# Sixty-four bytes: moving the norms' operands from 64 to 0 modulo 128 bytes in SBUF

## The chip, the cores and the metric

The kernel runs on 1 core of one Trainium2 chip. What counts is the device time of one execution in microseconds (us), lower being better. Engines are called TensorE (PE in the rows; PEld is its loading of stationary operands), VectorE (DVE), ScalarE (ACT), GpSimd (POOL) and SyncE (SP).

## The reference

Two transformer blocks over 256 tokens of width 1024, in float32. Block 1 has one layer: a mixer with three kinds of attention side by side, a gated MLP with a short convolution, and a gate on a second input `p`. Block 2 has two layers, each with a mixer (the first an mLSTM and stick-breaking attention, the second a gated delta network), a cross attention to a memory of 256 rows, and an MLP with a squared relu. Each part begins with an RMS norm with a gain.

```python
def first_block(x, p, ...):
    h = x
    hn = rms_norm(h, ln_mix[0])
    z = hn @ w_in[0]                       # split into q, k, v of 3 kinds of attention
    ...
    h = h + jnp.concatenate([o_a, o_b, o_c], axis=-1) @ w_out[0]
    h = h + conv_gated_mlp(rms_norm(h, ln_ffn[0]), w_up[0], conv_w[0], conv_b[0], w_down[0])
    gate = jax.nn.sigmoid(rms_norm(h, ln_ple[0]) @ w_ple_gate[0])
    return h + (p[0] @ w_ple_proj[0]) * gate

def second_block(x, mem, ...):
    memn = rmsnorm(mem, mem_norm)
    for l in range(2):
        h = rmsnorm(x, mix_norm[l])
        x = x + (ab_mixer(h, ...) if l == 0 else c_mixer(h, ...))
        x = x + mem_cross_attn(rmsnorm(x, xa_norm[l]), memn, xa_wq[l], xa_wk[l], xa_wv[l], xa_wo[l])
        x = x + sq_relu_mlp(rmsnorm(x, mlp_norm[l]), mlp_w1[l], mlp_w2[l])
    return rmsnorm(x, final_norm)
```

## The kernel before

All activations stay in SBUF, with features on the partitions: `h` is [128, 8, 256]. The weights (some 200 MB) stream in as chunks of 128 x 2048 floats (1 MB) in the order of their use. SyncE loads a chunk in two halves `raw`; ScalarE casts each into `hi` (float32r), VectorE or GpSimd makes the rest `lo` = raw - hi (`fetch`, line 433). A ring of three places holds `hi` and `lo`.

Every product of weights is made of three: hi x hi, hi x lo and lo x hi, each a product of 256 columns on a 128 x 128 stationary operand. A chunk is 48 such products. There are three ways to use a chunk:

- `gemm_a`: the weights are stationary, the activations move; result [columns, tokens] in a PSUM tile `pg`. In a trace its products read `pg<-oh,hi`, `pg<-ol,hi`, `pg<-oh,lo`: the moving operand stands first after the arrow, the stationary one second.
- `gemm_b`: the activations are stationary, the weights move; result [tokens, columns]: `pg<-hi,oh`, `pg<-lo,oh`, `pg<-hi,ol`.
- `gemm_c`: 256 rows of a weight, added up over the chunks in four tiles `acc`; the weights are stationary, the activations move: `acc<-oh,hi` and so on in the output projections, `acc<-mh,hi`, `acc<-mlo,hi` (`acc<-ml,hi` in block 1) in the MLPs' second products, `ph`/`plo` in `ple_p`.

The activations' two parts are `oh` and `ol`, 8 KB a partition each. `opnd` takes them from the pool `op` (two of each), for the norms' results, the memory's operand and the collected outputs of most mixers:

```python
    def opnd(self, pool=None):
        p = pool or self.op
        return (p.tile([128, 8, T], F32R, tag="oh", name="oh"), p.tile([128, 8, T], F32R, tag="ol", name="ol"))
```

Only the first mixer of block 2 takes its outputs' `oh` and `ol` from a pool of its own (line 1182, `ov = self.opnd(one)`), and there the gates' weights `gw` lie in that tile's first half too (line 1183); in the delta mixer (line 1382) both come from `op`.

In chunks, with an operand in `op`: attention of block 1 14, its output projection 4, gated MLP 22, last gate of block 1 4, first mixer of block 2 20, delta mixer 24 and its output projection 4, each cross attention 4 for queries and 4 for its output, each MLP of block 2 16. Of these 22 are used by `gemm_b`. The other chunks (the MLPs' second products, the first mixer's output projection, `ple_p`) move operands from other pools.

Order: TensorE runs its products in the order in which the program writes them. Attention and the recurrences are tasks that are written between the weights' products at places fixed by a table `W` of assumed times. The tile framework puts the other engines' work in order when the program is built.

Places: pools are stacked in SBUF in the order in which they are opened. The built program puts the tiles (bytes from the start of a partition) at:

```
pool            tiles              before              modulo 128
ring            hi, lo, raw        22720 to 88256      64
op              oh, ol             88256 to 121024     64
res             h                  121024 to 129216    64
sm              sq, u, R           129216 to 139456    64
later pools     mh, ml, mlo, ph,   from 140288         0
                plo, ov of ab_mixer
```

Of the kernel before, what the change touches and what calls it, by code (L numbers as in the profile page):

```python
# [19 lines left out]
# how long (us) a step beside the weight products waits for the other engines before the tensor engine takes it up  # L20
# [24 lines left out]
# ---------------------------------------------------------------- layout plan  # L45
def _plan():
    """Weight chunks of 128 x 2048 floats, in the order in which they are used."""
    ch = []

    def a(name, layer, cols):  # L50
        ch.append((name, layer, "A", cols))

    def c(name, layer, row):
        ch.append((name, layer, "C", row))

    idx = {}

    def mark(key):
        idx[key] = len(ch)

    sl = lambda s, n=256: [(s, n)]

    def kv(l, js):
        for j in js:
            for n in ("xa_wk_2", "xa_wv_2"):
                mark((n, l, j)); a(n, l, sl(256 * j))

    mark("va"); a("w_in", 0, sl(1024))
    for i in range(2):
        mark(("dqk", i, 0)); a("w_in", 0, [(128 * i, 128), (512 + 128 * i, 128)])  # L70
        mark(("dqk", i, 1)); a("w_in", 0, [(256 + 128 * i, 128), (768 + 128 * i, 128)])
    f0, c0 = 1280, 2438
    mark("vf0"); a("w_in", 0, sl(f0 + 768))
    for i in range(3):
        mark(("fqk", i)); a("w_in", 0, [(f0 + 128 * i, 128), (f0 + 384 + 128 * i, 128)])
        if i == 0:
            mark("vf1"); a("w_in", 0, [(f0 + 768 + 256, 128), (c0 + 768, 128)])
    for i in range(3):
        mark(("cqk", i)); a("w_in", 0, [(c0 + 128 * i, 128), (c0 + 384 + 128 * i, 128)])
        if i == 0:  # L80
            mark("vc1"); a("w_in", 0, sl(c0 + 768 + 128))
    for j in range(4):
        mark(("w_out", j)); c("w_out", 0, 256 * j)
    for j in range(22):
        mark(("w_up", j)); a("w_up", 0, [(128 * j, 128), (2816 + 128 * j, 128)])
        if j % 2 and j > 2:
            mark(("w_down", j // 2 - 1)); c("w_down", 0, 256 * (j // 2 - 1))
    mark(("w_down", 10)); c("w_down", 0, 2560)
    mark("ple_p"); c("w_ple_proj", 0, 0)
    for j in range(4):  # L90
        mark(("ple_g", j)); a("w_ple_gate", 0, sl(256 * j))
    kv(0, range(3))
    for j in range(2):
        mark(("mo", j)); a("ab_w_in_2", 0, sl(1024 + 256 * j))
    for j in range(2):
        mark(("sv", j)); a("ab_w_in_2", 0, sl(2568 + 256 * j))
    for h in range(4):
        mark(("sqk", h)); a("ab_w_in_2", 0, [(1544 + 128 * h, 128), (2056 + 128 * h, 128)])
    for j in range(2):
        mark(("mv", j)); a("ab_w_in_2", 0, sl(512 + 256 * j))  # L100
    for i in range(2):
        mark(("mqk", i)); a("ab_w_in_2", 0, [(128 * i, 128), (256 + 128 * i, 128)])
    kv(0, (3,))
    for j in (2, 3, 0, 1):
        mark(("ab_out", j)); c("ab_w_out_2", 0, 256 * j)
    for l in range(2):
        if l == 1:
            for g in range(2):
                for hh in range(4 * g, 4 * g + 4):
                    mark(("cqk2", hh)); a("c_w_in_2", 0, [(128 * hh, 128), (1024 + 128 * hh, 128)])  # L110
                for i in (2 * g, 2 * g + 1):
                    mark(("cv", i)); a("c_w_in_2", 0, sl(2048 + 256 * i))
            for j in range(4):
                if j == 3:
                    kv(1, range(4))
                mark(("cg", j)); a("c_w_in_2", 0, sl(3072 + 256 * j))
            for j in range(4):
                mark(("c_out", j)); c("c_w_out_2", 0, 256 * j)
        for j in range(4):
            mark(("xa_wq_2", l, j)); a("xa_wq_2", l, sl(256 * j))  # L120
        for j in range(4):
            mark(("xa_wo_2", l, j)); c("xa_wo_2", l, 256 * j)
        for j in range(16):
            mark(("w1", l, j)); a("mlp_w1_2", l, sl(256 * j))
            if j > 1:
                mark(("w2", l, j - 2)); c("mlp_w2_2", l, 256 * (j - 2))
        for j in (14, 15):
            mark(("w2", l, j)); c("mlp_w2_2", l, 256 * j)
    return ch, idx
# [15 lines left out]
# constants that depend on shapes alone: for the whole kernel, block 1, the first mixer  # L145
# [111 lines left out]
# ---------------------------------------------------------------- the program  # L257
class Task:
    """work beside the stream of weight products: a generator that yields how long its next step waits"""
# [5 lines left out]
class Prog:  # L265
    def __init__(self, ctx, tc, io):
# [3 lines left out]
        self.ring = pool("ring", 3)  # L270
        self.op = pool("op", 2)
        self.res = pool("res", 1)
# [14 lines left out]
    # -- order: the tensor engine runs what is traced as it is traced  # L287
# [14 lines left out]
    def wait(self, w):  # L302
        """a number, or the name of a wait: the next of its entries"""
        if not isinstance(w, str):
            return w or 0.0
        n = self.waits[w] = self.waits.get(w, -1) + 1
        v = W[w] if isinstance(W[w], tuple) else (W[w],)
        return v[min(n, len(v) - 1)]
# [6 lines left out]
    def queue(self, fn, wait=0.0, lanes=(0, 1)):  # L315
        """fn(lane) -> generator, when one of the lanes (two banks each) is free"""
        self.pend.append((fn, self.clk + self.wait(wait), lanes))
# [32 lines left out]
    # -- engines  # L350
# [32 lines left out]
    def three(self, out, l, r, start, stop):  # L383
        """a product of operands in two parts"""
# [9 lines left out]
    # -- banks  # L394
# [7 lines left out]
    def ps(self):  # L402
        """for work that is traced at one go"""
        self.psn = 1 - self.psn
        return self.bank(4 + self.psn)
# [26 lines left out]
    # -- weights  # L432
    def fetch(self, i, between=None):
        """the chunk's two parts; with between, in quarters, for the start"""
# [52 lines left out]
    def gemm_a(self, key, x):  # L487
        """[columns, tokens]: two tiles of columns"""
        return self.gemm_ab(key, x, False)

    def gemm_b(self, key, x):
        """[tokens, columns]: two tiles of tokens"""
        return self.gemm_ab(key, x, True)

    def gemm_c(self, key, xh, xl, acc, first, last, mid=None, banks=(0, 1, 2, 3)):
        """256 rows, accumulated over the chunks; with mid, the first 128 rows for all columns before it"""
# [14 lines left out]
    def gate_weights(self, i, w):  # L511
        """the gates' columns, two groups of heads at columns 0 and 32, as two parts side by side"""
# [8 lines left out]
    def gate_rows(self, x, w, out, tmp):  # L521
        """out [heads, groups, tokens] = the gates before their norm"""
# [10 lines left out]
    # -- norms: operands are h*g, the reciprocal root is applied to the products  # L533
# [4 lines left out]
    def split(self, x, k, src, n=1, eng=None):  # L538
        """x[:, k:k+n] = src (float32, SBUF or PSUM) as two parts"""
# [3 lines left out]
    def behind(self, last, pair):  # L543
        """the pair of instructions (of the scalar and the vector engine) comes after the names in last"""
# [11 lines left out]
    def norm(self, h, gain, add=None, cols=False, bank=None, pool_sq=()):  # L556
        """h (in place) += add; operands, R (broadcast over partitions) and R per token, whose task runs later"""
# [56 lines left out]
    def v_cols(self, dst, ps, rc):  # L614
        """dst(t) <- ps[:, t] * per token"""
# [3 lines left out]
    # ------------------------------------------------------------ setup  # L619
# [26 lines left out]
    def warm(self):  # L646
        """products that nothing uses, for the tensor engine's clock"""
# [5 lines left out]
    def last_norm(self, h, add, out):  # L653
        """the output: h += add, its norm, in tiles of two"""
# [29 lines left out]
    def log1pe(self, l, y, n):  # L684
        """l = ln(1 + exp(-|y|))"""
# [4 lines left out]
    # ------------------------------------------------------------ block 1  # L690
    def softmax(self, S, E, b0, b1, tag):
        """S: [q, 384] scores (128 keys of the first 128 queries, 256 of the others); E = exp(S + b - max); 1/sum"""
# [17 lines left out]
    def turn(self, pt, P):  # L710
        """P [q, 384] -> pt [keys, 384]"""
# [9 lines left out]
    def block1_attention(self, x, R, rc):  # L721
        nc, tc, io = self.nc, self.tc, self.io
        with ExitStack() as es:
# [94 lines left out]
            def post(key, gq_, gk_, then, bank):  # L818
                """the norms of a tile of queries and a tile of keys, then the attention with them"""
# [140 lines left out]
    def out_proj(self, keys, ov, tiles, there=None, halves=False):  # L960
        """the last chunk (or its second half) waits for all tasks"""
# [77 lines left out]
    # ------------------------------------------------------------ block 2  # L1039
# [19 lines left out]
    def mem_operand(self, x=None, last=None):  # L1059
        """the memory's operands"""  # L1060
# [8 lines left out]
    def kv(self, l, pool):  # L1069
        """keys and values of the memory; a closure for each head's chunks"""  # L1070
# [105 lines left out]
    def ab_mixer(self, x, R, rc, kv_head, *_):  # L1176
        nc, tc = self.nc, self.tc
        with ExitStack() as es:
# [13 lines left out]
            # gates of the mLSTM, heads on partitions  # L1192
# [12 lines left out]
            # output gates  # L1205
# [24 lines left out]
            # stick breaking  # L1230
# [46 lines left out]
            # mLSTM  # L1277
# [93 lines left out]
    def c_mixer(self, x, R, rc, kv_head, K, Vm):  # L1371
        nc, tc = self.nc, self.tc
        with ExitStack() as es:
# [7 lines left out]
            # the memory's operand, then the output's; the place of the memory's keys and values serves the convolutions before  # L1381
# [14 lines left out]
            def gates():  # L1396
                # beta and decays, heads on partitions
# [142 lines left out]
            def base(g, cpt):  # L1540
                # inverses of the 16 x 16 diagonal blocks, a block per partition
# [99 lines left out]
            def gated(j):  # L1641
                """heads 2 j, 2 j + 1: times their norms and gates, when both are there"""
# [59 lines left out]
    def blocks_out(self, N, cpt):  # L1702
        """N[(k b), r, c] = cpt[(b r), k, c]"""
# [4 lines left out]
    def blocks_in(self, ci, I):  # L1708
        """ci[(b r), k, c] = I[(k b), r, c]"""
# [62 lines left out]
```

## Time and profile before

| | |
|---|---|
| median of 3 runs | 1342.69 us (1340.6 to 1343.25) |
| profiled execution, its span | 1345.5 us; no other time of it is recorded |
| TensorE busy | 1280.4 us, 95% |
| VectorE, ScalarE, GpSimd busy | 924.7, 727.9, 274.7 us |
| weights' queue | 200.76 MB, 44.0% of the DMA engines' time |

The span runs from the first to the last instruction of the profiled execution. Busy time of TensorE counts overlapping products once. A product's own duration (some 0.28 us) runs from its start to the modelled end of its pipeline; the next product starts well before that end.

### The profile page before, as it was taken

The numbers are of one execution on the slowest core, as the hardware profiler recorded it, in microseconds if no ns is written. First come the engines' busy times: TensorE is split into PE (matmuls) and PEld (weight loads), VectorE is DVE, ScalarE is ACT, GpSimd is POOL, SyncE is SP. The second block draws the span as 40 slices with busy tenths as digits, with TensorE's granted clock in tenths as the row PEclk, the third lists the DMA queues.
The fourth block names the chain that finished last, engine by engine and source line by source line (L and its number), as shares of the span: only waits on it lengthen the run. The fifth ranks groups of instructions, "written<-read, shape, count | busy, mean of one in ns | idle before, by whom it ended". The sixth has DMA issues, their size and how long they took to land. (4 is left out here: it accounts for less than half of the span.)

```text
span 1345.5 us, 24944 instructions
## 1 busy us (share of the span) xinstructions
PE 1280.4 (95%) x10195; PEld 1238.7 (92%) x10195; DVE 924.7 (69%) x1401; ACT 727.9 (54%) x1217; POOL 274.7 (20%) x160
## 2 busy tenths in 40 slices
PE   8899989999999999999999999888898989999997
PEld 7788889999999999989999998778798989999997
DVE  7867687777786655686655657989685376755554
ACT  6665475655576554655444446564643564644442
POOL 4500330000223200262000015424214271100000
PEclk9999999999999999999999999999998989999999
DMA  8323445555565543434655555333234343455551
GB/s 267 135 98 108 140 165 188 177 182 182 181 205 185 173 152 128 155 130 140 211 180 184 182 184 170 137 92 109 94 110 131 110 141 122 161 188 186 183 184 45
DMA packets 65698, 208.40 MB, mean 155 GB/s; under 512 B 13192, under 2 KB 14752, under 8 KB 65584
## 3 DMA queue, kind: packets, MB, share of 16 engines
q1 hardware_dynamic: 56976, 200.76, 44.0%
q0 software_dynamic: 1600, 4.88, 1.1%
q10 hardware_dynamic: 7008, 1.18, 0.5%
q8 instruction: 80, 1.31, 0.4%
q14 instruction: 34, 0.28, 0.1%
HBM read 205.32 MB, written 1.44 MB: 154 GB/s over the span
## 5 line engine op out<-in xcount | busy, mean ns | idle before, releaser
L352 ACT ACTIVATE hi<-raw 128x1024 fp32r<-128x1024 f32 (+1 forms) x378 | 378.5, 1047 | 237.8 <-issue 101.9
L369 DVE TENSOR_TENSOR lo<-raw,hi 128x1024 fp32r<-128x1024 f32 (+1 forms) x311 | 378.2, 1250 | 171.7 <-ACT hi L352 171.3
L378 PE MATMUL pg<-oh,hi 128*128 128x256 f32 x1632 | 473.5, 290 | 9.2 <-DVE K L369 3.4
L378 PE MATMUL pg<-ol,hi 128*128 128x256 f32 x1632 | 466.2, 286 | 4.4 <-DVE ol L372 3.7
L378 PE MATMUL pg<-oh,lo 128*128 128x256 f32 x1632 | 464.0, 284 | 0.0
L378 PEld LDWEIGHTS pg<-oh,hi 128*128 128x128 f32 x1632 | 315.3, 193 | 14.2 <-issue 6.8
L378 PEld LDWEIGHTS pg<-ol,hi 128*128 128x128 f32 x1632 | 315.0, 193 | 10.1 <-DVE ol L372 8.3
L378 PEld LDWEIGHTS pg<-oh,lo 128*128 128x128 f32 x1632 | 315.0, 193 | 0.0
L369 POOL TENSOR_TENSOR lo<-raw,hi 128x1024 fp32r<-128x1024 f32 (+1 forms) x67 | 170.2, 2555 | 641.9 <-ACT hi L352 624.1
L378 PE MATMUL acc<-mh,hi 128*128 128x256 f32 x688 | 192.8, 280 | 0.6 <-ACT mh L352 0.6
L378 PE MATMUL acc<-mh,lo 128*128 128x256 f32 x688 | 192.0, 279 | 0.0
L378 PE MATMUL acc<-mlo,hi 128*128 128x256 f32 x512 | 142.8, 279 | 0.0
L378 PEld LDWEIGHTS acc<-mh,hi 128*128 128x128 f32 x688 | 129.3, 188 | 0.8 <-ACT mh L352 0.8
L378 PEld LDWEIGHTS acc<-mh,lo 128*128 128x128 f32 x688 | 129.3, 188 | 0.0
L378 PE MATMUL pg<-hi,oh 128*128 128x256 f32 x352 | 105.9, 301 | 5.4 <-DVE u L369 3.4
L378 PE MATMUL pg<-lo,oh 128*128 128x256 f32 x352 | 102.1, 290 | 1.5 <-DVE lo L369 1.4
L378 PE MATMUL pg<-hi,ol 128*128 128x256 f32 x352 | 101.8, 289 | 0.7 <-DVE ol L372 0.7
L378 PEld LDWEIGHTS acc<-mlo,hi 128*128 128x128 f32 x512 | 95.9, 187 | 0.0
L378 PE MATMUL acc<-oh,hi 128*128 128x256 f32 x320 | 91.6, 286 | 0.5 <-ACT oh L352 0.5
L378 PE MATMUL acc<-ol,hi 128*128 128x256 f32 x320 | 90.3, 282 | 0.1
L378 PE MATMUL acc<-oh,lo 128*128 128x256 f32 x320 | 90.2, 282 | 0.0
L369 POOL TENSOR_TENSOR sq<-sq 128x512 f32<-128x512 f32 (+1 forms) x20 | 26.7, 1337 | 261.8 <-ACT sq L352 260.5
(382 smaller groups left out, 1924.9 us busy)
## 6 DMA issues: line engine op xcount, KB each, us to landing
raw<-in_w SPq DMA_DIRECT2D x374, 512.0 KB, 4.2
mt<-in_memT POOLq DMA_DIRECT2D x12, 256.0 KB, 4.0
h<-in_xT SPq DMA_DIRECT2D x4, 256.0 KB, 4.9
raw<-in_w SPq DMA_DIRECT2D x4, 256.0 KB, 5.2
fl<-in_rel SPq DMA_DIRECT2D x3, 256.0 KB, 4.3
gw<-in_gw POOLq DMA_DIRECT2D x2, 256.0 KB, 2.9
out<-h SPq DMA_DIRECT2D x2, 256.0 KB, 2.7
con<-in_con SPq DMA_DIRECT2D x1, 384.0 KB, 7.0
```

The source lines that it names most:

```text
L352: return self.nc.scalar.activation(out, in_, func, **k)
L369: return (eng or self.nc.vector).tensor_tensor(out, a, b, op)
L378: i = self.nc.tensor.matmul(out, lhsT=l, rhs=r, start=start, stop=stop, skip_group_check=True)
```

## The change

Two tiles of 64 bytes a partition, each in a pool of its own, are allocated ahead of `op` and behind it. No instruction uses them. The rest of the change strips comments and docstrings, line for line, which moves nothing (and adds three lines ahead of line 274, so that later line numbers are 3 higher).

```diff
         self.cst = pool("cst", 1)
         self.ring = pool("ring", 3)
+
+        pool("gap0", 1).tile([128, 16], F32, name="gap0")
         self.op = pool("op", 2)
+        pool("gap1", 1).tile([128, 16], F32, name="gap1")
         self.res = pool("res", 1)
         self.sm = pool("sm", 2)
```

The places then are:

```
pool            tiles              after               modulo 128
ring            hi, lo, raw        22720 to 88256      64
op              oh, ol             88320 to 121088     0
res             h                  121152 to 129344    64
sm              sq, u, R           129344 to 139584    64
later pools     mh, ml, mlo, ...   from 140416         0
```

So `op` moves by 64 bytes, and everything behind it by 128. In the built programs each engine has the same instructions in the same order before and after.

## Rows read from the trace of the kernel before

**Rows 1.** Head of the page: busy us (share of the span) and instructions.
```profile
PE 1280.4 (95%) x10195; PEld 1238.7 (92%) x10195; DVE 924.7 (69%) x1401; ACT 727.9 (54%) x1217; POOL 274.7 (20%) x160
```

**Rows 2.** Busy time by stretch: attention, gated MLP, first mixer, MLP, delta mixer.
```profile
core 0: us, PE busy (x) PEld busy (x) DVE busy (x) ACT busy (x) POOL busy (x), PEclk, DMA share, GB/s
...
30.00:142.00 112.00, 106.71 (x750) 94.10 (x749) 83.36 (x193) 70.22 (x153) 23.58 (x16) 0.95 0.36 120
...
178.40:373.00 194.60, 191.79 (x1595) 190.55 (x1594) 154.03 (x229) 117.04 (x180) 19.05 (x15) 1.00 0.53 179
...
405.50:540.60 135.10, 135.10 (x1092) 132.74 (x1091) 78.03 (x103) 77.08 (x135) 17.60 (x9) 1.00 0.47 160
...
629.70:814.10 184.40, 183.82 (x1539) 183.16 (x1539) 112.58 (x124) 87.18 (x111) 15.51 (x8) 1.00 0.53 181
814.10:950.00 135.90, 116.98 (x869) 108.03 (x868) 120.09 (x206) 82.91 (x146) 56.18 (x27) 0.97 0.38 126
```

**Rows 3.** Waits of ScalarE: for whom, us in total, times, longest us.
```profile
ACT hi L352 <- PE pg L378: 93.9, 47, 9.0
```

**Rows 4.** Chain of waits, last MLP: start us, us, work, count.
```profile
1174.91 5.76 PE pg L378 x48
1180.67 5.66 PE acc L378 x48
```

**Rows 5.** Timeline of TensorE, output projection of the delta mixer: start us, us.
```profile
1068.03 0.28 PE L378 MATMUL acc<-oh,hi 128*128 128x256 f32 x1
...
1073.79 0.28 PE L378 MATMUL acc<-oh,hi 128*128 128x256 f32 x1
```

**Rows 6.** Timeline of TensorE, output projection of the first mixer.
```profile
550.16 0.28 PE L378 MATMUL acc<-oh,hi 128*128 128x256 f32 x1
...
551.93 0.28 PE L378 MATMUL acc<-oh,hi 128*128 128x256 f32 x1
```

**Rows 7.** Timeline of TensorE, weights moving, first mixer.
```profile
435.32 0.28 PE L378 MATMUL pg<-hi,oh 128*128 128x256 f32 x1
...
440.73 0.28 PE L378 MATMUL pg<-hi,oh 128*128 128x256 f32 x1
```

**Rows 8.** Timeline of TensorE, gates of the first mixer, then of the delta mixer.
```profile
441.08 0.28 PE L378 MATMUL ps<-oh 128*128 128x256 f32 x1
...
442.91 0.28 PE L378 MATMUL pg<-hi,oh 128*128 128x256 f32 x1
...
829.14 0.28 PE L378 MATMUL ps<-oh 128*128 128x256 f32 x1
...
830.77 0.28 PE L378 MATMUL pg<-oh,hi 128*128 128x256 f32 x1
```

**Rows 9.** Costliest groups of the page, loads: count, busy us, mean ns, idle before.
```profile
L378 PEld LDWEIGHTS pg<-oh,hi 128*128 128x128 f32 x1632 | 315.3, 193 | 14.2 <-issue 6.8
...
L378 PEld LDWEIGHTS acc<-mh,hi 128*128 128x128 f32 x688 | 129.3, 188 | 0.8 <-ACT mh L352 0.8
```

**Rows 10.** Groups of TensorE's products by operands: count, busy us, mean ns, idle.
```profile
L378 PE MATMUL pg<-oh,hi 128*128 128x256 f32 x1632 | 473.5, 290 | 9.2 <-DVE K L369 3.4 <-DVE u L369 2.6 <-DVE y L369 1.8
...
L378 PE MATMUL acc<-mh,hi 128*128 128x256 f32 x688 | 192.8, 280 | 0.6 <-ACT mh L352 0.6
...
L378 PE MATMUL acc<-mlo,hi 128*128 128x256 f32 x512 | 142.8, 279 | 0.0
L378 PE MATMUL pg<-hi,oh 128*128 128x256 f32 x352 | 105.9, 301 | 5.4 <-DVE u L369 3.4 <-ACT hi L352 1.1 <-ACT u L356 1.0
...
L378 PE MATMUL acc<-oh,hi 128*128 128x256 f32 x320 | 91.6, 286 | 0.5 <-ACT oh L352 0.5
...
L378 PE MATMUL acc<-ml,hi 128*128 128x256 f32 x176 | 49.3, 280 | 1.3 <-DVE ml L369 1.3
```

**Rows 11.** Groups of VectorE with shapes kept apart: count, busy us, mean ns, idle.
```profile
L372 DVE SCALAR_TENSOR_TENSOR cV<-cV,rq,u 128x128 f32<-128x128 f32 x16 | 4.6, 344 | 0.0
...
L372 DVE SCALAR_TENSOR_TENSOR om<-num,den,gg 128x128 f32<-128x128 f32 x8 | 2.2, 345 | 0.0
```

## The prediction

> **What bounds the kernel now.** The head of the page comes first: TensorE is busy 1280.4 of 1345.5 us, 95% [rows 1]. So the time is nearly that of one queue of products, and what one product takes is what counts. The stages then show where this holds without a gap. In the first MLP of block 2, its first mixer and the gated MLP of block 1 the busy time fills the stretch (183.82 of 184.40 us, 135.10 of 135.10, 191.79 of 194.60), while VectorE has 112.58, 78.03 and 154.03 us of work there. In the gated delta mixer it does not (116.98 of 135.90), and there VectorE is the busier one with 120.09; in the attention of block 1 TensorE has 106.71 of 112.00, at a granted clock of 0.95 [rows 2]. The weights are no limit: ScalarE's casts `hi` wait 93.9 us in total for products `pg`, that is for TensorE to free the three places of the ring, not the other way round [rows 3].
>
> Products overlap, so a row's own 0.28 us is not the price of a product; the distance from one start to the next is. The chain of waits, which merges unbroken work, gives it for a whole chunk: 48 products `pg` with the moving operand from `op` take 5.76 us, 120.0 ns each, and the 48 products `acc` of the chunks that follow take 5.66 us, 117.9 ns [rows 4]. Clock, shape (128x256 on a 128x128 stationary) and type are the same. The table of places in the section on the kernel gives one difference: in the first, both operands lie at 64 modulo 128; in the second, the moving one lies at 0 and the stationary one (the weights) at 64.
>
> **Is it the place, or the kind of product?** Four comparisons of the trace of before bear on it.
> First, the output projections. All run the same code. That of the delta mixer takes `ov` from `op` (64 against 64): from 1068.03 to 1073.79 us stand 48 products, 120.0 ns [rows 5]. That of the first mixer of block 2 takes `ov` from its own pool (0 against 64): from 550.16 to 551.93 stand 15, 118.0 ns [rows 6]. Same function, same weights' ring, 2 ns apart.
> Second, products in which the weights move and `oh` or `ol` is stationary (64 against 64): from 435.32 to 440.73 stand 45, 120.2 ns [rows 7].
> Third, the gates' products, moving `oh` and `ol` against a small weight tile. Where that tile lies in `op` (64 against 64), 14 take 1.63 us from 829.14, 116.4 ns; where it lies in the mixer's pool (64 against 0), 16 take 1.83 us from 441.08, 114.4 ns [rows 8]. Again 2 ns, and now it was the stationary operand that was moved.
> Fourth, the load of the stationary operand: 193 ns on average for `pg`, 188 for `acc` with `mh` [rows 9]. So it looks as if the load for the next product and the stream of the present one get in each other's way when they start at the same place modulo 128.
>
> The Trainium skill speaks against this: its page SBUF — State Buffer, section Who interferes with whom, gives TensorE two read ports, one for the moving operand and one for the load of weights, and calls them independent. By that the change would be worth nothing. Rows 5 and 6 differ by 2 ns all the same, and I go by the rows.
>
> **The change, part by part.** It adds no instruction and takes none away: both new tiles are written and read by nobody, and order and waits on every engine stay. What moves is `op` alone relative to everything else in the window of 128 bytes: `oh` and `ol` go from 64 to 0, while the ring, `h` and the later pools keep their place in it.
>
> Products that get faster: those with one operand in `op` and the other in the ring. The groups `pg` with `oh` or `ol` moving count 3 x 1632 = 4896, those with the weights moving 3 x 352 = 1056, and `acc` with `oh` or `ol` 3 x 320 = 960, less the 192 of the first mixer that already are at 0 [rows 10]. That is 6720, or 140 chunks of 48. Price: 5.76 - 5.66 = 0.10 us per chunk, so 14.0 us at most. For the 22 chunks in which the weights move, no row shows 64 against 0 with full-width loads; the nearest is the gates' 2.0 ns, so I price them like the others. Bounds for these 1056: nothing below (120 stays), and above, the gates' 114.4 ns, 5.8 ns each, 6.1 us instead of 2.2.
>
> Products that could get slower: the gates' 16 in the first mixer, now 0 against 0, cost 16 x 2 ns; nothing. The products `acc` with `mh`, `ml` or `mlo` keep 0 against 64 modulo 128, but every later pool moves by 128 bytes, so modulo 256 they change sides. They are 688 x 2 + 512 + 176 = 2064 [rows 10], with the first mixer's 192 and the 48 of `ple_p` 2304. Rows show no such pair, so the bounds are the ends seen: 114.4 and 120.2 ns against 117.9, from 8.1 us of gain to 5.3 us of loss. I take 0: the title's window is 128, and rows 8 show the same 2 ns from the other side of it.
>
> Other engines: 88 casts and as many subtractions of the norms write `op`, and VectorE reads `h` at 64 with `oh`, now at 0. Its product `om`, with inputs at 64 and 32, takes 345 ns, and `cV`, with both at 0, 344 [rows 11]; places that differ cost VectorE nothing.
>
> **What arrives at the end.** A chunk saved on TensorE counts only where TensorE is not waiting for others afterwards. By stages of [rows 2], in chunks with an operand in `op`:
> - gated MLP of block 1 (22) and the two MLPs of block 2 (16 each): 54 chunks with no wait to speak of; all of it, 5.4 us.
> - first mixer of block 2: 20 chunks, no gap at all; 2.0 us.
> - four output projections: 16 chunks, behind which the last attention steps are waited for; I take three quarters, 1.2 us.
> - attention of block 1 (14), its last gate (4), the queries of both cross attentions (8), the delta mixer (24): 50 chunks, 5.0 us. Here steps of VectorE and ScalarE are begun by one product and used by a later one; if the products between go faster, the later one waits longer by as much. TensorE idles in these stages already. I take half, 2.5 us.
> Sum 11.1 us; 2.9 of the 14.0 turn into longer waits for VectorE. The profiled execution has a span of 1345.5 us (no other time of it is known), which would become 1334.4. It lies 2.8 us above the median of the runs, 1342.7; from there the forecast is **1331.6 us**.
>
> **The rivals.**
> (a) No change. Either the reading ports don't meet, as the skill's page has it, or what makes `op` slow is its region and not its phase: it lies below byte 121,024, and all fast moving operands of other pools lie above 140,288. Rows 5 and 6 don't separate the two. Against the region: in rows 8 the moving operand is in `op` both times, and only the partner's place changes; but that partner also moves to the upper region. Then the time is 1342.7.
> (b) More than forecast. The 1056 products with weights moving fall to the gates' 114.4 ns (3.9 us more), and so may those of the later pools (8.1 us more): with the full 14.0 us, 1342.7 - 26.0 = 1316.7. For it speaks only that the gates' products, with half of their loads 64 wide, are quicker in every case (116.4 with equal places), so the level is more likely theirs alone.
> (c) Slower: the later pools. If 128 bytes put `mh`, `ml`, `mlo` and their like on a worse side against the weights, 2304 products pay. From 11.1 / 2304 = 4.8 ns each the gain is gone, and at 6 ns (the whole distance between the slowest and the fastest spacing seen) 13.8 us make 1345.4. The equal places cost only 2 ns, which speaks against it.
> (d) The gain is swallowed. All stages but the 54 plain chunks wait away what they save, and one of the gaps so lengthened brings the granted clock down once more. The 0.95 over 112.00 us stands for 5.6 us lost, in a stretch with waits [rows 2]; a third of that is 1.9. The time is then 1342.7 - 5.4 + 1.9 = 1339.2.
>
> **How the numbers follow.** A difference under about 0.2%, 2.7 us, is not told from none here. The forecast with its neighbours (4 to 18 us faster) gets 0.78; (a) 0.10; (b) 0.05; (c) 0.04; (d), as far as it eats nearly all, 0.03. Faster by over 0.2%: 0.78 + 0.05 and a little of (d), 0.84. Within: (a) and part of (c) and (d), 0.13. Slower: the rest of (c), 0.03. The range runs from the whole 14.0 us with 3.9 more for the moving weights (1324.8, so 1325) to (d) at 1339; outside it lie (a), most of (b) and (c), under two in ten.
>
> **What the profile after would show.** In the chain of waits, 48 products `pg` in 5.66 us like `acc`, or 5.76 if the step is wrong. The output projection of the delta mixer at 118 ns. Loads for `pg` at 188 instead of 193 ns. `acc` with `mh` still 5.66 us a chunk; more means (c). Longer waits of TensorE for VectorE in the delta mixer and the attention of block 1; the plain stretches shorter by 1.6 us for an MLP's 184.4 and 2.2 us for the gated MLP. The forecast is wrong if `pg` keeps its 120 ns, or if it reaches 118 and the waits grow by more than 2.9 us.

## The result and the profile after

The changed kernel takes 1332.56 us (median of 6 runs, 1327.06 to 1334.47), the kernel before in the same comparison 1342.97 us (1340.60 to 1348.09). The medians differ by 10.4 us; the ratio of the runs is 0.9911, 95% interval 0.9886 to 0.9936, which is some 12 us. Forecast were 11.1.

The profiled execution of the changed kernel is the fastest of its six (1327.06 us, span 1325.3). That of before has a span of 1345.5 us; since a span is 1.8 us shorter than the time in the runs that have both, it took some 1347.3 us (an estimate), 4.3 above its median. (The prediction set this span against a time, and so had 2.8; its forecast starts from the median and is not touched by it.) The two spans differ by 20.2 us, so stretches of the two traces differ by more than the medians do.

The head of the page, to [rows 1]: TensorE has 19.1 us less of busy time; every engine has the same number of instructions as before.

```profile
PE 1261.3 (95%) x10195; PEld 1220.8 (92%) x10195; DVE 922.0 (70%) x1401; ACT 727.8 (55%) x1217; POOL 276.1 (21%) x160
```

The chain of waits of the changed kernel in the last MLP, to [rows 4] (start us, us, work, count):

```profile
1150.46 5.65 PE acc L381 x48
1156.11 5.66 PE pg L381 x48
```

48 products `pg` take 5.66 us instead of 5.76; `acc` is where it was. The timeline of TensorE in the delta mixer's output projection, to [rows 5]: 36 products in 4.23 us, 117.5 ns instead of 120.0.

```profile
1055.09 0.28 PE L381 MATMUL acc<-oh,hi 128*128 128x256 f32 x1
...
1059.32 0.28 PE L381 MATMUL acc<-oh,hi 128*128 128x256 f32 x1
```

And with the weights moving, in the first mixer, to [rows 7]: 48 products in 5.44 us, 113.3 ns instead of 120.2.

```profile
440.89 0.28 PE L381 MATMUL pg<-hi,oh 128*128 128x256 f32 x1
...
446.33 0.28 PE L381 MATMUL pg<-hi,oh 128*128 128x256 f32 x1
```

The loads, to [rows 9]: 189 ns on average for `pg`, 193 before. Those of `acc<-mh,lo` went the other way, from 188 to 192 ns, though 48 products `acc` take 5.65 us as before. So a load's own duration does not follow the pace of the products. The first line is of before, the others of the changed kernel:

```profile
L378 PEld LDWEIGHTS acc<-mh,lo 128*128 128x128 f32 x688 | 129.3, 188 | 0.0
...
L381 PEld LDWEIGHTS pg<-oh,hi 128*128 128x128 f32 x1632 | 308.5, 189 | 11.9 <-issue 3.4 <-ACT hi L355 2.8 <-ACT K L359 1.8
...
L381 PEld LDWEIGHTS acc<-mh,lo 128*128 128x128 f32 x688 | 131.9, 192 | 0.0
```

Busy time by stretch of the changed kernel, each stretch from its stage's first product (columns as in [rows 2]): output projection of block 1, gated MLP, first mixer, queries and attention of the first cross attention with its projection, first MLP, delta mixer.

```profile
140.00:178.20 38.20, 32.83 (x241) 29.36 (x240) 24.76 (x50) 18.64 (x40) 9.83 (x5) 0.91 0.38 122
178.20:369.90 191.70, 189.30 (x1594) 188.06 (x1593) 152.98 (x227) 115.68 (x177) 19.34 (x15) 1.00 0.55 182
...
399.50:530.70 131.20, 131.20 (x1092) 128.86 (x1091) 80.90 (x106) 77.02 (x135) 20.05 (x10) 1.00 0.52 169
...
553.70:619.10 65.40, 60.97 (x501) 59.35 (x500) 47.43 (x60) 37.09 (x68) 32.89 (x18) 1.00 0.43 136
619.10:801.90 182.80, 182.06 (x1540) 181.41 (x1539) 112.67 (x124) 87.29 (x111) 15.62 (x8) 1.00 0.56 183
801.90:1041.10 239.20, 213.97 (x1643) 200.08 (x1642) 182.76 (x329) 127.12 (x247) 80.65 (x37) 0.97 0.39 119
```

Three of the same stretches of before that were not shown ahead:

```profile
142.80:178.40 35.60, 30.36 (x240) 27.16 (x239) 23.73 (x48) 16.97 (x36) 9.83 (x5) 1.00 0.38 130
...
564.20:629.70 65.50, 61.61 (x501) 60.00 (x500) 47.29 (x60) 36.93 (x68) 32.80 (x18) 1.00 0.41 136
...
814.10:1057.00 242.90, 216.37 (x1644) 202.15 (x1643) 184.35 (x329) 127.38 (x246) 81.84 (x37) 0.97 0.36 117
```

The MLP is shorter by 1.6 us, the gated MLP by 2.9, the first mixer by 3.9, the delta mixer by 3.7, the cross attention by 0.1. Block 1's output projection, with its attention's last steps, became 2.6 us longer; the granted clock there is 0.91, it was 1.00. A clock of 0.91 over 38.20 us stands for some 3.4 us lost (an estimate), more than those 2.6.

### The profile page after: what moved, and what is told of

Its sections match the earlier page's. It is cut to its first block, busy times and chain, and to the rows that moved or that the text cites. A ratio compares the mean times of both kernels' runs of the same rounds, so it can differ in the third digit from the quotient of the medians.

```text
span 1325.3 us, 24944 instructions
## 1 busy us (share of the span) xinstructions
PE 1261.3 (95%) x10195; PEld 1220.8 (92%) x10195; DVE 922.0 (70%) x1401; ACT 727.8 (55%) x1217; POOL 276.1 (21%) x160
## 5 line engine op out<-in xcount | busy, mean ns | idle before, releaser
L381 PE MATMUL pg<-oh,hi 128*128 128x256 f32 x1632 | 467.0, 286 | 7.1 <-DVE K L372 2.7
L381 PE MATMUL pg<-ol,hi 128*128 128x256 f32 x1632 | 459.3, 281 | 4.6 <-DVE ol L375 4.0
L381 PE MATMUL pg<-oh,lo 128*128 128x256 f32 x1632 | 457.5, 280 | 0.0
L381 PEld LDWEIGHTS pg<-oh,hi 128*128 128x128 f32 x1632 | 308.5, 189 | 11.9 <-issue 3.4
L381 PEld LDWEIGHTS pg<-ol,hi 128*128 128x128 f32 x1632 | 308.0, 189 | 9.9 <-DVE ol L375 8.5
L381 PEld LDWEIGHTS pg<-oh,lo 128*128 128x128 f32 x1632 | 308.7, 189 | 0.0
L372 POOL TENSOR_TENSOR sq<-sq 128x512 f32<-128x512 f32 (+1 forms) x20 | 27.5, 1375 | 255.9 <-ACT sq L355 254.6
```

The lines of the kernel that those rows point to most:

```text
L372: return (eng or self.nc.vector).tensor_tensor(out, a, b, op)
L381: i = self.nc.tensor.matmul(out, lhsT=l, rhs=r, start=start, stop=stop, skip_group_check=True)
```

## The experiments

All times are medians, all ratios against the kernel before on the same chip, with 95% intervals. Distances are those of the moving operand's place above the stationary one's, modulo 256 bytes; "later pools" means `mh`, `ml`, `mlo`, `ph`, `plo` and the first mixer's `ov`. Each of the first kernels is the kernel before with other gaps.

**1. Only the first gap.** `op` at distance 64, later pools at 128 (same place modulo 128 as the ring).

```diff
+        pool("gap0", 1).tile([128, 16], F32, name="gap0")
         self.op = pool("op", 2)
         self.res = pool("res", 1)
```

> Only the first gap: op goes to 0 modulo 128 as in the change, but h, sm and all later pools now move by 64, so mh, ml, mlo, ph, plo and the first mixer's ov lie at 64, like the weights' ring. Equal places are what costs: 48 products pg take 5.66 us as in the change, and 48 products acc with mh go from 5.66 to 5.76 us; 48 chunks (2304 products) pay 0.10 us each, so 4.8 us over the changed kernel, some 1337 us, about 0.996 of before. Rival, the region of op is what costs: acc with mh keeps 5.66 us, and the time is that of the change, about 1332.6 us.

Measured 1334.9 us, ratio 0.9931 (0.9909 to 0.9953), an interval that overlaps that of the change, so the time does not choose between the two expectations. The chain does. In its chain of waits (last MLP) `acc` with `mh` went up, but to 5.70 us, not to 5.76:

```profile
1163.03 5.65 PE pg L378 x48
1168.68 5.70 PE acc L378 x48
```

The region of SBUF is out as the only cause: `mh` moved by 64 bytes within its region, and its products slowed. But equal places modulo 128 cost less here than they do in `op`.

**2. Only the second gap.** `op` at distance 0, later pools at 128.

```diff
         self.op = pool("op", 2)
+        pool("gap1", 1).tile([128, 16], F32, name="gap1")
         self.res = pool("res", 1)
```

> Only the second gap: op stays at 64 modulo 128, the later pools go to 64. Equal places are what costs: pg keeps 5.76 us for 48 products and acc with mh goes from 5.66 to 5.76 us, so 4.8 us over before, about 1348 us, 1.0035 of before. Rival, region: nothing changes, 1343 us. A gain would speak against both.

Measured 1347.44 us, ratio 1.0020 (1.0002 to 1.0038): slower, by about half of what was expected. `acc` with `mh` went to 5.70 us, not to 5.76. The same two rows:

```profile
1205.36 5.70 PE acc L378 x48
1211.06 5.75 PE pg L378 x48
```

**3. A shift by 128.** `op` stays at 64 modulo 128, as before the change. Distance of `op` 128, of the later pools 192.

```diff
+        pool("gap0", 1).tile([128, 32], F32, name="gap0")
         self.op = pool("op", 2)
```

> One gap of 128 bytes ahead of op: op and all that follows move by 128 and keep their places modulo 128; modulo 256 they change sides. If the place modulo 128 decides: pg 5.76, acc with mh 5.66 us for 48 products, time as before, 1343 us. If the place modulo 256 decides (op then at 64, ring at 192): pg falls to 5.66 or less, time 1332 us.

Measured 1329.59 us, ratio 0.9887 (0.9862 to 0.9911): as fast as the change. This is where the theory of the prediction fell: with both operands at 64 modulo 128, `pg` goes from 5.76 to 5.70 us (5.66 or less was expected of a window of 256), and `acc` with `mh`, whose place modulo 128 has not moved either, from 5.66 to 5.47.

```profile
1161.04 5.70 PE pg L378 x48
1166.74 5.47 PE acc L378 x48
```

**4. Distance 32.** `op` at 32, later pools at 192.

```diff
+        pool("gap0", 1).tile([128, 8], F32, name="gap0")
         self.op = pool("op", 2)
+        pool("gap1", 1).tile([128, 24], F32, name="gap1")
```

> Gaps of 32 and 96 bytes: op lies at 96 modulo 128, 32 behind the ring's 64; all else as in the change. If any unequal place will do: pg 5.66 us for 48 products and about 1332 us. If only places 64 apart keep out of each other's way: pg 5.76 us and 1343 us. Profile of the change showed two spacings for unequal places, 113.3 and 117.8 ns; if the distance chooses between them, pg with 113.3 throughout gives 48 x 4.5 ns = 0.21 us a chunk less than the change on up to 140 chunks, down to 1303 us.

Measured 1324.98 us, ratio 0.9849 (0.9822 to 0.9876); run again on another chip 1325.58 us, 0.9847. `pg` takes 5.60 us, a value that none of the three expectations named, and `acc` 5.46:

```profile
1167.86 5.60 PE pg L378 x48
1173.46 5.46 PE acc L378 x48
```

`acc` with `mh` has distance 192 here, as in the change, where it takes 5.65. So the distance alone does not fix the spacing.

**5. The distances by themselves.** A kernel that leaves out all the rest: products on zeros in `gemm_a`'s order, two chunks of 48 for each distance d.

```python
    ...
    for order in (range(0, 512, 32), range(480, -1, -32)):
        for d in order:
            group(d)
            group(d)
    for d in range(0, 512, 16):
        nc.scalar.activation(o, bank, AF.Copy)
        group(d)
        group(d)
    ...
```

> Products alone, on zeros, 48 to a chunk in the order of gemm_a, with the moving operand's place d bytes above the stationary one's, d from 0 to 511; the rest of the computation is left out. First d in steps of 32 upwards and downwards without a pause, then in steps of 16 after a pause each. If the distance modulo 256 decides: 120.0 ns at 0 and 256, about 118.7 at 128 and 384, 113.3 or 117.8 at 64, 113.3 at 192, and the same at d and d + 256. If modulo 128: the same at d and d + 128. If what went before decides between two spacings: different values for the same d going up, going down and after a pause.

Products in stretches of 5.00 us, all within the second chunk at a distance: 0, 64, 96, 128 and 192 on the way up, 192, 96 and 64 on the way down, 112 after a pause, and at last 448 on the way down (us from and to, length, busy us with the count of products, clock, then DMA share and GB/s). The counts take in two or three products that began before the stretch: 44 stands for 120.0 ns from start to start, 45 for 117.8 or 118.6, 47 for 113.3.

```profile
43.65:48.65 5.00, 5.00 (x44) 1.00 0.00 0
66.38:71.38 5.00, 5.00 (x45) 1.00 0.01 3
77.78:82.78 5.00, 5.00 (x44) 1.00 0.00 0
89.24:94.24 5.00, 5.00 (x45) 1.00 0.00 0
111.67:116.67 5.00, 5.00 (x47) 1.00 0.01 3
326.53:331.53 5.00, 5.00 (x45) 1.00 0.00 0
360.73:365.73 5.00, 5.00 (x44) 1.00 0.00 0
371.93:376.93 5.00, 5.00 (x47) 1.00 0.00 0
493.42:498.42 5.00, 5.00 (x47) 1.00 0.00 0
...
236.20:241.20 5.00, 5.00 (x47) 1.00 0.00 0
```

The distance from start to start, ns, mean over the second chunk (worked out from the starts in the trace of one execution):

```
distance     0     32     64     96    128    160    192    224    256
going up   120.0  117.8  117.8  120.0  118.6  117.3  113.3  118.3  120.0
going down 120.0  116.7  113.3  120.0  118.6  118.6  117.8  118.3  120.0
pause      120.0  116.7  117.8  120.1  118.7  118.7  117.8  118.4  120.0
```

In steps of 32, the same levels come back from 256 to 511; which of two is taken at 320, 416 and 448 was not always as at 64, 160 and 192. So the window is 256 bytes at these steps, the middle of it (128) is not the equal of 0, 96 is as bad as 0, and 64 and 192 have two spacings, 117.8 and 113.3 ns. The steps of 16 between were run after a pause only: 113.3 at 112 and at 368, but 118.7 at 16 against 113.3 at 272. Whether 16 has two spacings too was not tested.

The distance of the chunk before does not settle which one is taken. On the way down 192 came after 224 and took 117.8; 448 came after 480, the same two distances modulo 256, and took 113.3. There 128, 96 and 64 in turn ended at 113.3, and 384, 352 and 320 at 117.8. Whether a longer history or a window longer than 256 tells them apart was not separated.

**6. Which of the two?** Three kernels: both groups 64 below the ring (`op` 192, later pools 192); the change with the later pools put back to 64; `op` 192 with the later pools at 64.

The first of the three:

```diff
+        pool("gap0", 1).tile([128, 48], F32, name="gap0")
         self.op = pool("op", 2)
+        pool("gap1", 1).tile([128, 48], F32, name="gap1")
```

The second has gaps of 16 and 48 elements of 4 bytes in these places, the third 48 and 16.

> Gaps of 192 and 192 bytes: op and the later pools both lie 64 bytes below the weights' ring modulo 256 (128 against 192). The runs before showed that acc with mh at that distance took 113.3 to 114 ns a product beside pg at 32 or 128, but 117.8 beside pg at 64. Theory, the distance modulo 256 decides and minus 64 is the quick side: pg and acc both near 113.5 ns, 5.45 us for 48; against the change 0.21 us on some 166 chunks of weights used as stationary operand, 35 us, of which a quarter is lost to waits: some 1306 us. Rival, either side of 64 has two spacings and nothing chooses between them: 117.8 in the MLPs, 1332 us. A window of 128, as the prediction had it: no difference from the change, 1332 us.

> op as in the change (64 above the ring modulo 256), the later pools at 64 above it too, where they were before (gaps of 64 and 192 bytes). It tells what the move of the later pools by 128 was worth in the change. If nothing: time of the change, 1332 us, and 5.66 us for 48 products of either kind. If the later pools' side carried part of the gain: slower than the change by that part, up to 5 us.

> op 64 below the ring modulo 256, the later pools 64 above it (gaps of 192 and 64 bytes). If the quick spacing goes with minus 64 for each kind of chunk by itself: pg 5.45 us, acc with mh 5.66 us, about 1332 - 118 x 0.21 x 0.75 = 1313 us. If the spacing once reached goes on through the chunks that follow: acc with mh falls to 5.45 us too, about 1306 us, or pg stays at 5.66, 1332 us.

Measured 1330.96 us, 0.9894 (0.9871 to 0.9918); 1332.57 us, 0.9910 (0.9883 to 0.9937); 1330.39 us, 0.9884 (0.9862 to 0.9906). The intervals of all three overlap that of the change. The gains that the first and the third might have had over the change did not come: in the last MLP all three chains stand at the slow one of the two spacings, as these rows show, two of the kernel with both at 192 and two of the one with `op` at 192 and the later pools at 64.

```profile
1160.62 5.65 PE pg L378 x48
1166.27 5.65 PE acc L378 x48
...
1155.92 5.65 PE pg L378 x48
1161.58 5.66 PE acc L378 x48
```

The middle one answers a rival of the prediction: the move of the later pools by 128 was worth nothing in the change that these runs can tell, since with them put back the ratio is 0.9910 against 0.9911, each within 0.3%.

**7. Pairs of distances.** Again products alone: a chunk as in `gemm_a` at distance a, one as in `gemm_c` at b, three times, then a copy by ScalarE. That copy was meant to make a pause and made none: it needs the first kind of chunk alone and runs beside the second.

```python
    ...
    for a in range(0, 256, 32):
        for b in range(0, 256, 32):
            nc.scalar.activation(o, bank, AF.Copy)
            for n in range(3):
                up(a)
                down(b, n == 0, n == 2)
    ...
```

> Products alone, on zeros, in the order of an MLP: a chunk as in gemm_a with its moving operand a bytes above the stationary one, then a chunk as in gemm_c with b bytes, three times, then a pause, for a and b from 0 to 224 in steps of 32; the rest of the computation is left out. If the distance of each chunk alone sets its spacing: the sum of two chunks' times is that of the rows of the run with distances (5.76 at 0 and 96, 5.69 at 128, 5.65 or 5.44 at 64 and 192, 5.60 at 32, 5.63 at 160, 5.68 us at 224). If the chunk before decides which of the two spacings is taken: a 192 after 32, 128 or 160 takes 5.44 us, after 64 it takes 5.65 us, as in the runs of the whole kernel; the pair with the smallest sum is then the one to build.

This was one execution. Idle time of TensorE before the chunks as in `gemm_a`, at the end of the row: 12.8 us before the first product of all and 0.7 for the copies, of which there are 64. So but for the first the 64 pairs of distances ran on without a break.

```profile
L1730 PE MATMUL bank<-x,w 128*128 128x256 f32 x9264 | 1125.6, 281 | 13.5 <-ACT x L1724 12.8 <-ACT o L1758 0.7
```

The middle one of three pairs, us for the two chunks (worked out from the starts in the trace):

```
a, b        kernel with these in its MLPs   both chunks   a      b
0, 64       before                          11.42         5.76   5.66
64, 192     the change                      11.31         5.66   5.65
64, 128     only the first gap              11.35         5.66   5.70
128, 192    shift by 128                    11.17         5.70   5.47
32, 192     distance 32                     11.06         5.60   5.46
192, 32     not yet built                   11.06         5.46   5.60
0, 128      only the second gap             11.45         5.75   5.70
64, 64      change, later pools back        11.31         5.65   5.65
192, 192    both at 192                     10.88         5.44   5.44
192, 64     op 192, later pools 64          11.10         5.45   5.65
```

All but the last two agree with the chains of the whole kernels to 0.02 us a pair; those two are at the quick spacing here and at the slow one there (11.30 and 11.31 us). In every case a chunk at 192 took 5.44 to 5.47 us right behind one at 0, 32, 128 or 160, here and, for 32 and 128, in the whole kernels. Behind 64 it took either: 5.65 us as the second chunk of the pair 64, 192 (the first row below) and 5.45 as the first chunk of 192, 64 (the second row, between two chunks at 64), but 5.65 again with these two distances in the whole kernel. Behind 96 it was 5.65 as the second and 5.45 to 5.46 as the first. 192 behind 192 was quick here and slow in the whole kernel.

```profile
787.50:792.50 5.00, 5.00 (x45) 1.00 0.00 0
...
1735.00:1740.00 5.00, 5.00 (x47) 1.00 0.00 0
```

So what ran earlier than the chunk before has a part in it, or else the order of the products in the two kinds of chunk; this was not separated.

**8. The version that this points to.** `op` at 192, the later pools at 32, beside the change and the kernel with distance 32 on one chip.

```diff
+        pool("gap0", 1).tile([128, 48], F32, name="gap0")
         self.op = pool("op", 2)
+        pool("gap1", 1).tile([128, 8], F32, name="gap1")
```

> op 64 below the ring modulo 256, the later pools 32 above it (gaps of 192 and 32 bytes): the run with pairs gave 5.46 and 5.60 us to the two chunks of an MLP in this order, 11.06 for both, against 11.31 in the change and 11.42 before. Theory, the chunk with 32 sends the next one at minus 64 to its quick spacing: 113.7 ns for pg and 116.7 for acc with mh in all three MLPs, 0.25 us on 43 pairs and more in the chains of pg alone, so some 12 us under the change less a quarter for waits, about 1322 us. Rival, the pauses of the whole kernel put it back into the slow spacing as with both at minus 64: about 1330 us.

> The changed kernel as it is, beside the two others on one chip: 0.991 of before, about 1332 us.

> op 32 above the ring, the later pools 64 below it, as in the run with gaps of 32 and 96 bytes, on the same chip as the two others: 0.985 of before, about 1325 us. If that run was only a lucky one: no different from the change.

Measured 1317.84 us, ratio 0.9799 (0.9768 to 0.9830); the change 1329.54 us, 0.9881 (0.9849 to 0.9913); distance 32 1325.58 us, 0.9847 (0.9812 to 0.9882). For the first, about 1322 was expected. Its chain in the last MLP holds the quick spacing for `pg`:

```profile
1160.75 5.46 PE pg L378 x48
1166.21 5.60 PE acc L378 x48
```

It has the lowest median of this study: 27.5 us under before and 11.7 under the change, with no instruction added. Its interval lies clear of that of the change and overlaps that of distance 32.

## Why the prediction was right, and where it was not

- **TensorE is the bound, and a chunk saved on it arrives.** Right. In the stretches without waits the gain arrives: 1.6 us for the MLP as forecast, 2.9 for the gated MLP (2.2 forecast), of which 2.5 are busy time.
- **5.66 us for 48 products `pg`.** Right for nearly all of the 118 chunks with activations moving: 5.66 in the MLPs, 117.5 ns in the output projection. Some took the quick spacing: by the starts in the trace, among others the last three such chunks before 405 us, in the last gate of block 1 and at the start of the first mixer, ran at 113.3 ns.
- **It is the place, not the region or the kind of product.** Right; experiments 1 to 3 move the place within a region and the spacing follows, and experiment 5 has the same two tiles at all distances. The Trainium skill (SBUF — State Buffer, Who interferes with whom) calls TensorE's two read ports independent; by that there would have been no change, and the trace disagrees: the same products on zeros take 120.0 ns at distance 0 and 113.3 to 117.8 at 64. That the load and the stream get in each other's way, as the prediction guessed, is not shown: the loads' own durations do not follow the pace.
- **"The title's window is 128."** Wrong, and so are the comparisons "64 against 64" as the prediction put them. What decides repeats every 256 bytes (in the steps of 32 of experiment 5). In the kernel before the operands in `op` lay at distance 0 modulo 256, the worst place; the change put them to 64. Had `op` been 128 away, equal places by the prediction's window, it would have started from 118.6 ns and not from 120.0, and experiment 3 shows a gain with the place modulo 128 kept. The number came out right because 64 is off 0 in either window, which is luck.
- **22 chunks with the weights moving at the price of the others.** Mis-sized. After the change their distance is 192, and where they reach the quick spacing they take 5.44 us, 0.32 less than before, not 0.10. By the starts in the trace six in ten of these products did, and the mean is 115.3 ns; the prediction had this only as its bound (114.4 ns). The first mixer, which has 10 of them, gained 3.9 us instead of 2.0.
- **The later pools at 0.** Right (experiment 6), but for a reason that the prediction did not have: 192 could have given 113.3, and beside chunks at 64 it stayed at 117.8. In the trace above only the first mixer's own outputs left it: by the starts, 126 of their 192 products ran at 113.3. Taken together with the other distances, this term was worth up to 0.2 us a chunk.
- **2.9 us lost to longer waits.** Not borne out. TensorE's idle time, its span less its busy time, is 65.1 us before and 64.0 after, and 66.5 in the profile of the changed kernel in experiment 8 (span 1331.4, busy 1264.9). The delta mixer, of which half was written off, kept 3.7 us, and its longest wait for VectorE became shorter in total, as the rows below show (us in total, times, longest; before, then after). Block 1's output projection lost 2.6, for which its lower clock alone would do (the 3.4 above).
- **The sum, 11.1 us.** In part luck. By the distances from start to start in the two traces (an estimate) the products that the prediction named saved some 18 us and not 14.0: 11.7 instead of 10.2 for the 102 chunks of `gemm_a`, 4.7 instead of 2.2 for the 22 of `gemm_b`, 2.1 instead of 1.6 in the output projections. Too low a price and a loss that was not seen stand against each other in the sum. The measured gain is 10.4 us between the medians of the first comparison and 15.8 between those of experiment 8, so the runs do not fix it closely enough to test a term of 2.9; why it came out smaller than the products' 18 us stays open.

```profile
PE pg L378 <- DVE u L369: 6.0, 4, 2.1
...
PE pg L381 <- DVE u L372: 4.9, 4, 2.3
```

What stays open: why a chunk at 64 or 192 takes one spacing or the other. That the distance alone does not fix it, and that what ran before has a part in it, is shown. After the pauses of experiment 5, 64, 192, 320 and 448 all took the slow one. What in TensorE's loads and streams holds a spacing is not seen in any record.

## What to carry to other kernels

Where TensorE streams 256-column float32r products with a load of weights for each, look at the distance of moving and stationary operand in SBUF modulo 256 bytes: here the same 48 products took 5.44 to 5.76 us. Shift pools with unused tiles, and try pairs of distances for chunks that alternate, in the whole kernel too, since two of the ten pairs in the table of experiment 7 ran at another pace there than alone. Take the starts of products from the trace, not their durations, which stayed at 0.28 us throughout. And when two rows differ in a place, work out the place in more than one window before naming the window.

## What the runs showed that was not expected

Two stable spacings at one distance, 117.8 and 113.3 ns, with what looks like a memory that lasts for hundreds of products: in the whole kernel with both at 192 the last MLP stood at 5.65 us a chunk throughout, while the same pair among products alone stood at 5.44. Distance 96 is as slow as 0 (120.0 ns), and 112 next to it was 113.3 (run after a pause only).
